# A chain of token mixers and feed-forward layers: the delta rule on raw keys and queries, a plain first chunk, wide projections

## The chip, the cores and the metric

The kernel runs on one core of one Trainium2 chip. The metric is the time of one execution on the device, in microseconds. Before the change it is 2003.51 us, the median of three runs (1998.67 to 2003.72).

## What is computed

The input is x, 256 tokens of 1024 channels in float32. Two layers of a first block are followed by two of a second block; each step is added to x after an RMS norm:

```python
for l in range(2):                       # first block
    x += 0.5 * swiglu(norm(x), ffa_w_in[l], ffa_w_out[l])          # d_ff = 2816
    x += mix(norm(x) @ w_in[l])          # MLA, gated delta rule (GDN), MoBA; gated sum @ w_out
    x += 0.5 * swiglu(norm(x), ffb_w_in[l], ffb_w_out[l])
for l in range(2):                       # second block
    x += even_mixer(norm(x)) if l == 0 else odd_mixer(norm(x))
    x += conv_glu(norm(x))               # silu(conv3(h @ w_gate)) * (h @ w_up) @ w_down
```

The delta rule has 4 heads of 128 and chunks of 64 tokens. q and k are normalised to length 1 (q is also scaled by 128 ** -0.5):

```python
a   = strict_lower((k * beta) @ k.T * decay)        # 64 x 64 in each chunk and head
u,w = solve(I + a, [v * beta, k * beta * exp(gcum)])
qk  = q @ k.T * decay
for each chunk: v_new = u - w @ state
                o     = (q * exp(gcum)) @ state + qk @ v_new
                state = state * exp(g_last) + (k * exp(g_last - gcum)).T @ v_new
o = rms_norm(o, out_norm) * silu(z)
```

The odd mixer has a linear recurrent unit (LRU) with a gelu gate, and dilated attention over 3 dilations and 4 heads of 64.

## The kernel before, in words

**Weights and products.** Weights come from HBM in chunks of up to 1 MB, one DMA each on SP's queue, into three staging buffers (`chunk`, L252). ScalarE rounds each piece of 1024 columns to a high part (L279) and VectorE subtracts for the low part (L280), into three buffers each. Every product with a weight is a sum of three: high*high, high*low, low*high. There are two forms:

- plain (`mm3`, L285; called by `gather_T` and `gather_nat`): three matmuls of 256 columns to one PSUM bank. `gather_T` makes channels by tokens, `gather_nat` tokens by channels, with x as the stationary operand and the weight's columns (256, or 212) as the moving one.
- paired (`gather_pair`, L405): x's high and low part stand side by side, so one matmul of 512 columns (L414) and one of 256 (L416) replace the three. The result lies in two halves of two banks; `whole` (L524) adds them with two ScalarE copies (L527) and two VectorE additions (L529).

PSUM has eight banks in two pools of four: `pa` for products with weights, `ps` for all else.

**Norms.** The update of x by a layer also makes the next layer's split x (`xx`, L361) and its squares. `stats` (L378) turns the sum of squares into 1/rms by a chain of small VectorE instructions (`rsqrt`, L311, three Newton steps) and spreads it over partitions with TensorE (`rows`, L343), as R. Results of products are multiplied by R afterwards, so the first products of a layer do not wait for it.

**Feed-forward** (`ffn`, L515). Eleven chunks of 256 channels: gate product, R, silu, up product, then the split into `gx`. The four swiglu layers use the paired form for gate and up, the two conv layers the plain one for gate and the paired one for up. `stats` comes after the first up product.

**The first block's mixer** (`mixer`, L658). The order in the program comes from generators: each `yield` is a step, and `_mix(main, fill, ratio)` (L185) puts `ratio` steps of filler behind each step of the main work. The order of each engine's queue follows from the program's order and a simulated timeline; only in the part from L727 is TensorE's order as written. The stages:

1. `mla_c` (L782): two products of 212 columns.
2. MLA's projections and heads, with `fill` (convolutions and projections of the GDN, gates) and `moba_proj` (L908: six products of 256 columns) as filler.
3. MoBA's four pairs of heads (`heads`, L613: logits `pL`, softmax, transposes `pPT`, output `pOT`), with what is left of `fill`, then `merge` of branch 0, then `gdn_keys` woven with the gates of branch 2 as filler, at 2.05 steps of filler for one (L697 to L709).
4. `gdn_invert` (L1124, the inverse of I + a in six levels), with `gdn_rest` woven with gates and merges as filler; `gdn_solve`; `gdn_scan` (L1202).

`gdn_keys` (L1026) turns the raw keys to tokens by channels (`pgk`), squares and sums them, makes 1/norm, multiplies (`kn`, L1046), transposes the normalised keys back (`pgkT`), copies them out (`knT`, L1051), and multiplies them with themselves (`pA`, L1073) and with the decay `Dn`, which holds beta. `gdn_rest` (L1076) does the same with the queries (`pgq`, `rsqrt`, `qn` L1099, `pgqT`, `gqT` L1111, `pQK`), and makes the right-hand sides `vb`, `kbe`, the state's keys `kde`, and the decayed queries (GpSimd L1112, `pgqd`).

**The odd mixer** (`odd`, L1436). Queries, keys and values take nine products of 256 columns (`qkv`, L1483). They are mixed with the LRU and with the transposes of q and k (`turn`). `dil_attn` (L1556: logits `pdL`, softmax, 18 transposes `pdPT` for each of two pairs, output `pdo`) then has the LRU's gate (`plg`) and the first two chunks of the output product (`pr`) as filler, at 0.3.

Of the kernel before, what the change touches and what calls it, by code (L numbers as in the profile page):

```python
# [40 lines left out]
def _rows(chunks, *kts):  # L41
# [9 lines left out]
    "w_in": _rows([[(0, 212)], [(212, 416), (1952, 1960)]]  # L51
                  + _runs((2472, 4008), (416, 1952), (1960, 2472), (4008, 7080)), 8),
# [8 lines left out]
    "od_w_in_2": _rows(_runs((0, 3328)), 8),  # L61
# [157 lines left out]
class _Net:  # L219
# [222 lines left out]

    def Rb(self, n=2, R=None):
        return (self.R if R is None else R).unsqueeze(1).to_broadcast([128, n, S])
# [70 lines left out]
    def ffn(self, gate, up, down, layer, scale, gain, conv=None):  # L515
        nc = self.nc
        v2 = lambda a: a.rearrange("p (b s) -> p b s", b=2)
        with ExitStack() as ctx:
# [13 lines left out]
            for c in range(11):  # L532
                if conv is None:
                    pg = self.proj_pair(*gate(c), self.pa, "pg")
                else:
                    pg = _all(self.proj_T(*gate(c), "pg"))
                if c == 0:
                    pu = self.proj_pair(*up(c), self.ps, "pu")
                    self.stats()
                if conv is None:  # L540
# [20 lines left out]
                g = whole(pu, "g")  # L561
                nc.vector.scalar_tensor_tensor(g, th, 0.5, g, op0=OP.mult, op1=OP.mult)
# [95 lines left out]
    def mixer(self, l, gain):  # L658
        pool = lambda ctx, name, bufs, **kw: ctx.enter_context(
            self.tc.tile_pool(name=name, bufs=bufs, reuse_waits="tile", **kw))  # L660
        with ExitStack() as ctx:
# [5 lines left out]
            with ExitStack() as c2:  # L667
# [29 lines left out]
                def keys():  # L697
                    yield from f
                    yield from self.merge(l, big, mg, 0, got["gate0"], brs[0])
                    yield from _weave(prep(), self.gates(l, big, got["gate2"], 2, 0))  # L700

                def prep():
                    got["D"] = self.gdn_decay(gk, got["scal"])
                    got["keys"] = yield from self.gdn_keys(gk, at, got[1], got["D"][0])
# [5 lines left out]
            with ExitStack() as c2:  # L710
                gp = pool(c2, "mxg", 1)
                scal = got["scal"]
                kn, knT, A = got["keys"]
# [3 lines left out]
                us = tiles("us")  # L717

# [8 lines left out]
                with self.tc.manual_schedule(engines={mybir.EngineType.PE}):  # L727
                    with ExitStack() as c3:
                        wk = pool(c3, "mxh", 1)
                        side = self.gdn_rest(out, wk, got, scal, got["D"][1], kn, knT)  # L730
# [4 lines left out]
                    with ExitStack() as c3:  # L735
                        brs[1] = _mix(self.gdn_scan(big, pool(c3, "mxj", 2), scal, out, us, got["sz"]), rest, 1.5)
# [45 lines left out]
    def mla_c(self, l, big):  # L782
        nc = self.nc
        csb = big.tile([128, 2, 424], F32, name="csb")
        ps = [_all(self.proj_nat("w_in", 28 * l + c, 212, "pc")) for c in range(2)]
        self.stats()
        for c in range(2):
            for t in range(2):
                nc.scalar.activation(csb[:, t, c * 212:(c + 1) * 212], ps[c][:, t * 212:(t + 1) * 212], AF.Copy,
                                     scale=self.rc[:, t:t + 1])  # L790
# [117 lines left out]
    def moba_proj(self, l, z):  # L908
        for i in range(3):
            for c in range(2):  # L910
                p = yield from self.proj_nat("w_in", 28 * l + W_MOBA + 2 * i + c, 256, "pmq")
                self.nat_heads(z[i][:, :, c * 256:(c + 1) * 256], p, 256)
# [70 lines left out]
    def gdn_decay(self, gp, scal):  # L983
# [16 lines left out]
        nc.vector.tensor_tensor(Dn, Dn, bc(beta), op=OP.mult)  # L1000
# [25 lines left out]
    def gdn_keys(self, gk, at, raw, Dn):  # L1026
# [3 lines left out]
        bch = lambda a: a.unsqueeze(2).to_broadcast([128, 4, 128])  # L1030
        ss = self.tiny.tile([128, 8], F32, tag="ss8", name="ss8")
        ps, kn, knT, A = [], [], [], []
        for t in range(2):
            ps.append(self.transposes("pgk", lambda h: raw[:, h, t * 128:(t + 1) * 128]))
# [4 lines left out]
        nc.vector.tensor_scalar(ss, ss, 0.25, EPS, op0=OP.mult, op1=OP.add)  # L1039
        r = self.rsqrt(ss, 8, "rl2")  # L1040
        nc.vector.tensor_scalar(r, r, 0.5, None, op0=OP.mult)
        for _ in range(4):
            yield
        for t in range(2):
            kn.append(gk.tile([128, 512], F32, name=f"kn{t}"))
            nc.vector.tensor_tensor(h4(kn[t]), h4(ps[t]), bch(r[:, 4 * t:4 * t + 4]), op=OP.mult)  # L1046
            yield
        for t in range(2):
            p = self.transposes("pgkT", lambda h: kn[t][:, h * 128:(h + 1) * 128])
            knT.append(gk.tile([128, 512], F32, name=f"knT{t}"))  # L1050
            nc.scalar.activation(knT[t], p, AF.Copy)  # L1051
            yield
        for t in range(2):
            p = self.ps("pA")
            self.inner(p, knT[t], knT[t])
# [4 lines left out]
        return kn, knT, A  # L1060
# [7 lines left out]
    def inner(self, p, a, b):  # L1068

        for h in range(4):  # L1070
            for c in range(2):
                s = slice(h * 128 + c * 64, h * 128 + c * 64 + 64)
                self.nc.tensor.matmul(p[64 * c:64 * c + 64, h * 64:h * 64 + 64], a[:, s], b[:, s],  # L1073
                                      start=True, stop=True)

    def gdn_rest(self, out, wk, raw, scal, Dt, kn, knT):  # L1076
# [3 lines left out]
        wq, kbe, kde, vb, qkT = out  # L1080
        h4 = lambda a: a.rearrange("p (h s) -> p h s", h=4)
        bch = lambda a: a.unsqueeze(2).to_broadcast([128, 4, 128])
        W = lambda nm: wk.tile([128, 512], F32, tag="gw", bufs=2, name=nm)
        f = self.tiny.tile([128, 2, 2, 4], F32, tag="gf", name="gf")
        ss = self.tiny.tile([128, 8], F32, tag="ss8", name="ssq")
        ps = []
        for t in range(2):
            ps.append(self.transposes("pgq", lambda h: raw[0][:, h, t * 128:(t + 1) * 128]))
            junk = W("gj")
            nc.scalar.activation(junk, ps[t], AF.Square)  # L1090
            nc.vector.reduce_sum(ss[:, 4 * t:4 * t + 4], h4(junk), axis=AX)
            yield
        nc.vector.tensor_scalar(ss, ss, 0.25, EPS, op0=OP.mult, op1=OP.add)
        r = self.rsqrt(ss, 8, "rq")
        nc.vector.tensor_scalar(r, r, 0.5 * 128 ** -0.5, None, op0=OP.mult)
        qn = []
# [631 lines left out]
```

## Time and profile before

| | |
|---|---|
| median of three runs | 2003.51 us |
| the profiled execution | 1998.36 us |
| its span, first to last instruction | 1996.6 us |
| TensorE busy | 1958.7 us (98%) |
| VectorE, ScalarE, GpSimd busy | 1537.9, 1102.9, 128.8 us |
| read from HBM | 323.87 MB |

A matmul's row has the length from its issue to its modelled end, with the pipeline in it; the distance between the starts of two matmuls that follow one another is what one costs in a full stream. An idle time is named behind the instruction that ended it, with what released it.

### The profile page before, as it was taken

What the parts mean: (1) busy time and instruction counts of PE and PEld (TensorE: products, weight loads), DVE (VectorE), ACT (ScalarE), POOL (GpSimd) and SP (SyncE); (2) the same over time, 40 slices, a digit from 0 to 9 for tenths busy, and PEclk for the clock granted to TensorE, in tenths of its full rate; (3) what the DMA queues carried; (4) which work ended last, traced back from release to release, by engine and by line L of the source; (5) the groups of instructions that cost most, each with busy time, mean ns of one, the idle gap of its engine ahead of it and who ended that gap; (6) DMA issues with size and microseconds to landing.
All of it is one profiled execution on the core that took longest, in us unless ns stands there. A gap on an engine that the chain in (4) does not pass through costs nothing.

```text
span 1996.6 us, 35914 instructions
## 1 busy us (share of the span) xinstructions
PE 1958.7 (98%) x14452; PEld 1799.1 (90%) x14452; DVE 1537.9 (77%) x2841; ACT 1102.9 (55%) x1812; POOL 128.8 (6%) x158
## 2 busy tenths in 40 slices
PE   7999999999999999999998999999999999999999
PEld 6889999799888988899997998889999999989998
DVE  6776899747877677768996587766978876978875
ACT  5555666435555555546663355555645655666653
POOL 0000030220000000001203100000000000020000
PEclk9999999999999999999999999999999999999999
DMA  6555544224555555555331255555244555426554
GB/s 239 190 185 186 175 148 148 105 66 158 180 190 179 194 176 190 181 186 180 130 146 69 102 172 187 184 180 185 106 148 169 190 177 201 168 63 220 183 179 137
DMA packets 50695, 327.24 MB, mean 164 GB/s; under 512 B 6624, under 2 KB 8672, under 8 KB 18528
## 3 DMA queue, kind: packets, MB, share of 16 engines
q1 hardware_dynamic: 49296, 324.09, 46.4%
q8 instruction: 113, 1.85, 0.4%
q10 hardware_dynamic: 1232, 0.85, 0.1%
q14 instruction: 54, 0.44, 0.1%
HBM read 323.87 MB, written 1.05 MB: 163 GB/s over the span
## 4 chain that ended last, share of the span: by engine, by line
PE 94%; DVE 3%; ACT 2%; issue 1%; DMA 0%; SPq 0%; DVEq 0%; ACTq 0%
PE pu L414 12%; PE pr L414 9%; PE pg L414 8%; PE pu L416 6%; PE pr L416 5%; PE pg L416 4%; PE pr L289 3%; PE pr L290 3%; PE pr L288 3%; PE pga L288 2%; PE pg L290 2%; PE pg L288 2%; PE pg L289 2%; PE pga L290 2%; PE pga L289 2%; PE pb L288 1%
## 5 line engine op out<-in xcount | busy, mean ns | idle before, releaser
L279 ACT ACTIVATE whi<-st 128x1024 fp32r<-128x1024 f32 (+2 forms) x628 | 651.0, 1037 | 695.4 <-PE pr L414 121.2
L280 DVE TENSOR_TENSOR wlo<-st,whi 128x1024 fp32r<-128x1024 f32 (+2 forms) x628 | 756.6, 1205 | 316.6 <-ACT whi L279 310.6
L414 PE MATMUL pu<-xx,whi 128*128 128x512 f32 x1056 | 372.5, 397 | 0.0
L416 PE MATMUL pu<-xx,wlo 128*128 128x256 f32 x1056 | 290.4, 280 | 0.0
L414 PE MATMUL pr<-gx,whi 128*128 128x512 f32 x792 | 272.7, 395 | 0.0
L414 PE MATMUL pg<-xx,whi 128*128 128x512 f32 x704 | 250.1, 399 | 11.3 <-ACT whi L279 11.3
L414 PEld LDWEIGHTS pu<-xx,whi 128*128 128x128 f32 x1056 | 196.3, 188 | 43.0
L416 PE MATMUL pr<-gx,wlo 128*128 128x256 f32 x792 | 211.2, 279 | 0.0
L416 PEld LDWEIGHTS pu<-xx,wlo 128*128 128x128 f32 x1056 | 199.4, 189 | 2.8
L416 PE MATMUL pg<-xx,wlo 128*128 128x256 f32 x704 | 194.4, 281 | 1.1 <-DVE wlo L280 1.1
L414 PEld LDWEIGHTS pr<-gx,whi 128*128 128x128 f32 x792 | 144.4, 188 | 29.7
L414 PEld LDWEIGHTS pg<-xx,whi 128*128 128x128 f32 x704 | 131.6, 189 | 41.2 <-ACT whi L279 12.0
L416 PEld LDWEIGHTS pr<-gx,wlo 128*128 128x128 f32 x792 | 149.3, 189 | 5.4
L416 PEld LDWEIGHTS pg<-xx,wlo 128*128 128x128 f32 x704 | 133.6, 190 | 4.7 <-DVE wlo L280 2.7
L288 PE MATMUL pga<-xx,whi 128*128 128x256 f32 x384 | 112.7, 293 | 0.0
L288 PE MATMUL pg<-xx,whi 128*128 128x256 f32 x384 | 109.3, 285 | 1.0 <-ACT whi L279 1.0
L290 PE MATMUL pg<-xx,wlo 128*128 128x256 f32 x384 | 109.3, 285 | 0.8 <-DVE wlo L280 0.8
L289 PE MATMUL pg<-xx,whi 128*128 128x256 f32 x384 | 109.1, 284 | 0.0
L289 PE MATMUL pga<-xx,whi 128*128 128x256 f32 x384 | 108.8, 283 | 0.0
L290 PE MATMUL pga<-xx,wlo 128*128 128x256 f32 x384 | 108.6, 283 | 0.0
L288 PEld LDWEIGHTS pg<-xx,whi 128*128 128x128 f32 x384 | 73.7, 192 | 2.2 <-ACT whi L279 1.2
L288 PEld LDWEIGHTS pga<-xx,whi 128*128 128x128 f32 x384 | 73.3, 191 | 2.4 <-issue 1.0
(563 smaller groups left out, 4547.2 us busy)
## 6 DMA issues: line engine op xcount, KB each, us to landing
st<-in_w_in_dram SPq DMA_DIRECT2D x52, 1024.0 KB, 4.8
st<-in_ffb_w_in_dram SPq DMA_DIRECT2D x44, 1024.0 KB, 4.8
st<-in_ffa_w_in_dram SPq DMA_DIRECT2D x43, 1024.0 KB, 4.9
st<-in_ffn_w_gate_dram SPq DMA_DIRECT2D x22, 1024.0 KB, 4.8
st<-in_ffn_w_up_dram SPq DMA_DIRECT2D x22, 1024.0 KB, 4.8
st<-in_ffa_w_out_dram SPq DMA_DIRECT2D x16, 896.0 KB, 4.5
st<-in_ffb_w_out_dram SPq DMA_DIRECT2D x16, 896.0 KB, 4.5
st<-in_ffn_w_down_dram SPq DMA_DIRECT2D x16, 896.0 KB, 4.6
```

Of the source, the lines that this page charges most:

```text
L279: self.hi = nc.scalar.activation(hi[:, :m], s, AF.Copy).ins
L280: nc.vector.tensor_tensor(lo[:, :m], s, hi[:, :m].bitcast(F32), op=OP.subtract)
L288: mm(out, a[0], b[0], start=start, stop=False, **kw)
L289: mm(out, a[0], b[1], start=False, stop=False, **kw)
L290: mm(out, a[1], b[0], start=False, stop=stop, **kw)
L414: mm(p, hi[:, k, c], x.rearrange("p e s -> p (e s)"), start=first == k0 + k, stop=False, skip_group_check=True)
L416: mm(p[:, S:], lo[:, k, c], x[:, 0, :], start=False, stop=last == k0 + k, skip_group_check=True)
```

## The change

- **Delta rule.** Keys and queries are no longer normalised. `a` and `qk` are products of the raw, transposed convolution results; 1/|k|^2 * beta multiplies the rows of `Dn`, 1/|k| * beta goes into `vb`, 1/|k|^2 * beta * exp(gcum) into `kbe`. The queries' length goes into the epsilon of the output's norm (`vq`, two small matmuls and a copy). The transposes `pgkT` and `pgqT` with their copies, the products L1046 and L1099, the queries' `rsqrt` and GpSimd's L1112 go; a copy of the raw keys (`kr`), a reciprocal, and a product out of PSUM for the decayed queries (`qd`) come. `inner` runs before the query transposes.
- **Order in stage 3.** `gdn_keys` is woven with merge 0 and then the gates, and not with the gates alone.
- **Plain first chunk.** Chunk 0 of each `ffn` uses the plain form for gate and up (six up products and four gate products), into one `pa` bank each.
- **Wide projections.** `wide_nat` makes 424 or 512 columns at a time, one bank for each half of the tokens: for `mla_c`, `moba_proj` and two of three products of each `qkv`. Weights are laid out in chunks of 4 rows of blocks by 512 columns.
- **Odd mixer.** The LRU's gate is mixed with the transposes of k; the values' products move into the filler of `dil_attn`, at 1.0, and must be done before its first output product.

The diff, cut to its core:

```diff
+    def wide_nat(self, name, i, cols, nm="pn"):
+        ps = [self.pa(nm) for _ in range(2)]
+        for j in range(2):
+            for k0, kk, hi, lo in self.chunk(name, i + j):
+                for t in range(2):
+                    for k in range(kk):
+                        m = 4 * j + k0 + k
+                        x = [a[:, t * 128:(t + 1) * 128] for a in self.xs(m)]
+                        self.mm3(ps[t][:, :cols], x, (hi[:, k, :], lo[:, k, :]), m == 0, m == KD - 1)
+                    yield
+        return ps
...
             for c in range(11):
-                if conv is None:
+                pair = conv is None and c > 0
+                if pair:
                     pg = self.proj_pair(*gate(c), self.pa, "pg")
                 else:
                     pg = _all(self.proj_T(*gate(c), "pg"))
                 if c == 0:
-                    pu = self.proj_pair(*up(c), self.ps, "pu")
+                    pu = _all(self.proj_T(*up(c), "pu"))
                     self.stats()
...
                     yield from f
-                    yield from self.merge(l, big, mg, 0, got["gate0"], brs[0])
-                    yield from _weave(prep(), self.gates(l, big, got["gate2"], 2, 0))
+                    yield from _weave(prep(), _chain(self.merge(l, big, mg, 0, got["gate0"], brs[0]),
+                                                     self.gates(l, big, got["gate2"], 2, 0)))
...
-        ps = [_all(self.proj_nat("w_in", 28 * l + c, 212, "pc")) for c in range(2)]
+        ps = _all(self.wide_nat("w_in", 28 * l, 424, "pc"))
...
-            for c in range(2):
-                p = yield from self.proj_nat("w_in", 28 * l + W_MOBA + 2 * i + c, 256, "pmq")
-                self.nat_heads(z[i][:, :, c * 256:(c + 1) * 256], p, 256)
+            ps = yield from self.wide_nat("w_in", 28 * l + W_MOBA + 2 * i, 512, "pmq")
...
     def gdn_keys(self, gk, at, raw, Dn, beta):
...
-            nc.scalar.activation(junk, ps[t], AF.Square)
+            nc.scalar.activation(junk, p, AF.Square)
+            nc.scalar.activation(kr[t], p, AF.Copy)
             nc.vector.reduce_sum(ss[:, 4 * t:4 * t + 4], h4(junk), axis=AX)
             yield
-        r = self.rsqrt(ss, 8, "rl2")
...
-            nc.vector.tensor_tensor(h4(kn[t]), h4(ps[t]), bch(r[:, 4 * t:4 * t + 4]), op=OP.mult)
-            yield
-        for t in range(2):
-            p = self.transposes("pgkT", lambda h: kn[t][:, h * 128:(h + 1) * 128])
...
+        nc.vector.tensor_scalar(ss, ss, 4 * EPS, None, op0=OP.add)
+        nc.vector.reciprocal(r2, ss)
+        nc.vector.tensor_tensor(r2, r2, fl(beta), op=OP.mult)
+        nc.vector.tensor_tensor(Dn, Dn, r2.unsqueeze(2).to_broadcast([128, 8, 64]), op=OP.mult)
+        yield
         for t in range(2):
             p = self.ps("pA")
-            self.inner(p, knT[t], knT[t])
+            self.inner(p, raw, raw, t)
...
+        r = self.rsqrt(ss, 8, "rl2")
+        nc.vector.tensor_tensor(rb, r, fl(beta), op=OP.mult)
...
     def gdn_rest(...):
+        for t in range(2):
+            p = self.ps("pQK")
+            self.inner(p, raw[1], raw[0], t)
...
+            p = self.transposes("pgq", lambda h: raw[0][:, h, t * 128:(t + 1) * 128])
+            nc.scalar.activation(junk, p, AF.Square)
+            nc.vector.tensor_tensor(h4(qd[t]), h4(p), bch(egc[:, t, :]), op=OP.mult)
...
+        p = self.ps("pvq")
+        for c in range(2):
+            nc.tensor.matmul(p[half(c), 0:8], self.ident[:, half(1 - c)], ss, start=True, stop=True)
+        nc.vector.tensor_copy(vq, p[:, 0:8])
...
     def odd(self, gain):
             _mix(qkv(0, q), core, 0.5)
-            for i, z in ((1, k), (2, v)):
-                turned = turn(i - 1, (q, k)[i - 1], (qT, kT)[i - 1])
-                _mix(qkv(i, z), _chain(turned, core), (0, 0.5, 0.2)[i])
-                _all(turned)
+            turned = turn(0, q, qT)
+            _mix(qkv(1, k), _chain(turned, core), 0.5)
+            _all(turned)
             _all(core)
-            fill = _chain(lru_gate(), lru_out())
-            _mix(self.dil_attn(wk, dil, qT, kT, v, yh, yl, (q, k)), fill, 0.3)
+            turned = turn(1, k, kT)
+            _mix(lru_gate(), turned, 0.5)
+            _all(turned)
+            values = qkv(2, v)
+            fill = _chain(values, lru_out())
+            _mix(self.dil_attn(wk, dil, qT, kT, v, yh, yl, (q, k), values), fill, 1.0)
```

## Rows read from the trace of the kernel before

**Rows 1.** The page: engines' busy time, and the chain that ended last.

```profile
PE 1958.7 (98%) x14452; PEld 1799.1 (90%) x14452; DVE 1537.9 (77%) x2841; ACT 1102.9 (55%) x1812; POOL 128.8 (6%) x158
...
PE 94%; DVE 3%; ACT 2%; issue 1%; DMA 0%; SPq 0%; DVEq 0%; ACTq 0%
```

**Rows 2.** Waits of TensorE: who waited for whom, total us, times, longest.

```profile
PE pA L1073 <- ACT knT L1051: 6.3, 3, 3.0
...
PE pT L1136 <- DVE qn L1099: 1.2, 1, 1.2
PE prow L348 <- DVE rc L389: 1.1, 2, 0.5
```

**Rows 3.** Timeline of TensorE, plain form and mla_c: 256 columns, then 212.

```profile
198.81 0.28 PE L288 MATMUL pr<-gx,whi 128*128 128x256 f32 x1
198.93 0.28 PE L289 MATMUL pr<-gx,whi 128*128 128x256 f32 x1
...
199.17 0.26 PE L288 MATMUL pc<-whi,xx 128*128 128x212 f32 x1
...
209.88 0.52 PE L383 MATMUL pst<-ones,sqacc 128*128 128x1 f32 x4
210.25 0.36 PE L288 MATMUL pga<-xx,whi 128*128 128x256 f32 x1
```

**Rows 4.** Timeline of TensorE: 512 columns, and a step of the paired form.

```profile
247.58 0.40 PE L289 MATMUL pkv<-wlo,ch 128*128 128x512 f32 x1
247.81 0.40 PE L290 MATMUL pkv<-whi,cl 128*128 128x512 f32 x1
...
711.50 0.40 PE L414 MATMUL pg<-xx,whi 128*128 128x512 f32 x1
...
711.85 0.40 PE L414 MATMUL pg<-xx,whi 128*128 128x512 f32 x1
```

**Rows 5.** Timeline of TensorE, end of stage 3, layer 0.

```profile
370.84 0.92 PE L300 MATMUL pL<-qkT 64*128 64x128 f32 x6
...
374.71 1.04 PE L1065 MATMUL pgkT<-C,kn 128*128 128x128 f32 x8
378.75 0.69 PE L1073 MATMUL pA<-knT 128*64 128x64 f32 x16 [3.00 <-ACT knT L1051]
...
382.08 1.27 PE L602 MATMUL pPT<-C,pr 128*128 128x128 f32 x6
384.01 0.43 PE L297 MATMUL pOT<-PT,mv 128*64 128x256 f32 x1 [0.65 <-ACT PT L604]
...
384.81 0.39 PE L1136 MATMUL pF<-C,gF 64*64 64x64 f32 x6
```

**Rows 6.** Timeline of ScalarE in the same stretch.

```profile
376.80 0.47 ACT L604 ACTIVATE PT<-pPT 128x384 f32<-128x384 f32 x1
```

**Rows 7.** Windows: granted clock (PEclk) after the waits; columns us, engines, PEclk, DMA.

```profile
379.53:382.94 3.41, 3.19 (x28) 2.48 (x29) 1.12 (x3) 0.55 (x2) 2.25 (x4) 0.50 0.00 0
...
1062.20:1065.60 3.40, 3.31 (x40) 2.56 (x40) 1.67 (x3) 1.04 (x3) 1.35 (x2) 0.50 0.02 5
...
1512.80:1516.10 3.30, 3.30 (x18) 3.30 (x17) 0.00 (x0) 0.00 (x0) 0.00 (x0) 0.50 0.07 30
...
1773.90:1788.40 14.50, 11.34 (x98) 8.34 (x96) 10.54 (x23) 10.22 (x25) 2.78 (x2) 1.00 0.19 55
```

**Rows 8.** Chain that ended last: one group of four transposes in gdn_rest.

```profile
402.57 0.59 PE pgqT L1065 x4
```

**Rows 9.** Timeline, second chunk of a swiglu and of conv_glu: waits of TensorE.

```profile
30.32 0.73 PE L414 MATMUL pg<-xx,whi 128*128 128x512 f32 x2 [1.03 <-ACT whi L279]
...
31.58 0.38 PE L416 MATMUL pg<-xx,wlo 128*128 128x256 f32 x1 [0.52 <-DVE wlo L280]
...
1510.58 0.39 PE L288 MATMUL pg<-xx,whi 128*128 128x256 f32 x1 [1.03 <-ACT whi L279]
...
1511.84 0.39 PE L290 MATMUL pg<-xx,wlo 128*128 128x256 f32 x1 [0.76 <-DVE wlo L280]
```

More of the change, by code (lines that the diff above doesn't have):

```diff
@@ L60 @@
     "ev_w_out_2": [(c, (k, 4)) for k in (0, 4) for c in _OUT],
-    "od_w_in_2": _rows(_runs((0, 3328)), 8),
+    "od_w_in_2": _rows(_runs((0, 1024)), 8)
+                 + [x for c in range(1024, 3328, 768)
+                    for x in _rows([[(c, c + 512)]], 4, 4) + _rows(_runs((c + 512, c + 768)), 8)],
     "od_w_out_2": [(c, (k, n)) for k, n in ((0, 4), (4, 2)) for c in _OUT],
@@ L537, in ffn @@
                 if c == 0:
-                    pu = self.proj_pair(*up(c), self.ps, "pu")
+                    pu = _all(self.proj_T(*up(c), "pu"))
                     self.stats()
-                if conv is None:
+                if conv is None and not pair:
+                    zz = wk.tile([128, 2, S], F32, tag="z", name="z")
+                    nc.vector.tensor_tensor(zz, v2(pg), self.Rb(), op=OP.mult)
+                elif pair:
                     zz = whole(pg, "z")
@@ L712, in mixer @@
                 scal = got["scal"]
-                kn, knT, A = got["keys"]
+                kr, rs, A = got["keys"]
                 tiles = lambda nm, n=512: [gp.tile([128, n], F32, name=f"{nm}{t}") for t in range(2)]
@@ L729, in mixer @@
                         wk = pool(c3, "mxh", 1)
-                        side = self.gdn_rest(out, wk, got, scal, got["D"][1], kn, knT)
+                        side = self.gdn_rest(out, wk, got, scal, got["D"][1], kr, rs, vq)
                         M = _mix(self.gdn_invert(pool(c3, "mxi", 2), A), _weave(side, rest), 0.65)
@@ L1059, in gdn_keys @@
             yield
-        return kn, knT, A
+        r = self.rsqrt(ss, 8, "rl2")
+        nc.vector.tensor_tensor(rb, r, fl(beta), op=OP.mult)
+        yield
+        return kr, (r2, rb), A
     def transposes(self, nm, src):
@@ L1066, in transposes, with inner, gdn_rest @@
         return p
-    def inner(self, p, a, b):
+    def inner(self, p, a, b, t):
         for h in range(4):
             for c in range(2):
-                s = slice(h * 128 + c * 64, h * 128 + c * 64 + 64)
-                self.nc.tensor.matmul(p[64 * c:64 * c + 64, h * 64:h * 64 + 64], a[:, s], b[:, s],
+                s = slice(t * 128 + c * 64, t * 128 + c * 64 + 64)
+                self.nc.tensor.matmul(p[64 * c:64 * c + 64, h * 64:h * 64 + 64], a[:, h, s], b[:, h, s],
                                       start=True, stop=True)
-    def gdn_rest(self, out, wk, raw, scal, Dt, kn, knT):
+    def gdn_rest(self, out, wk, raw, scal, Dt, kr, rs, vq):
         nc = self.nc
@@ L1486, in qkv @@
                 for g in range(3):
-                    p = yield from self.proj_nat("od_w_in_2", 4 + 3 * i + g, 256, "pd")
-                    self.nat_heads(z[:, g], p, 256)
+                    if g == 0:
+                        ps = yield from self.wide_nat("od_w_in_2", 4 + 3 * i, 512, "pd")
+                        for t in range(2):
+                            nc.scalar.activation(z[:, 0:2, t, :], v2(ps[t]), AF.Copy, scale=self.rc[:, t:t + 1])
+                    elif g == 2:
+                        p = yield from self.proj_nat("od_w_in_2", 6 + 3 * i, 256, "pd")
+                        self.nat_heads(z[:, g], p, 256)
                     if i == 2:
@@ L1602, in dil_attn @@
                     yield
+            _all(values)
             po = self.ps("pdo")
```

102 lines of the change are left out of this document (43 added, 59 removed).

## The prediction, made before the changed kernel ran

> **What bounds the kernel now.** The page first: TensorE is busy for 98% of the span, and the chain that ended last runs through it for 94% [rows 1]. So the time is TensorE's work, plus the places where it waits. VectorE (77%) and ScalarE (55%) count only where TensorE waits for them, and DMA has no share in the chain: the bytes stay the same, so transfers are costed at nothing, covered by products that outlast them. Next, the waits of TensorE: few and short, but the longest of the ones inside the kernel belong to the part that changes, 6.3 us for `knT`, then 1.2 for `qn` and 1.1 for `rc` [rows 2]. Last, the timeline, for what one matmul costs (distance between starts): 0.12 us for 256 columns, and (209.88 - 199.17) / 96 = 0.112 for 212 [rows 3]; 0.23 for 512, and 0.35 for a paired step, which does the work of three plain matmuls [rows 4]. The price goes with columns, so fewer, wider matmuls save little each.
>
> The sum below is made against the profiled execution, 1998.4 us. The median of the three runs shown is 5.1 us above it; I keep that distance. What a measurement of this kernel can tell from no change is 0.3%, 6 us.
>
> **The change, part by part.**
>
> *Wide projections.* `mla_c`: 96 matmuls of 0.112 become 48 of 424 columns. Between 256 columns at 0.12 and 512 at 0.23 a straight line gives 0.194 (bounds: 0.193 at the price per column of 512, 0.199 at that of 256) [rows 3, 4]. So 10.7 - 9.3 = 1.4 us a layer (1.2 to 1.5). `moba_proj`: 288 matmuls of 0.12 become 144 of 0.233, 1.0 us a layer; the odd mixer's three pairs of narrow products lose as much, 1.0. Sum 2 x 2.4 + 1.0 = -5.8. The number of DMAs, pieces and splits stays; evacuations get fewer, and lie under products. Two banks are now held at once, of four in `pa`; nothing else uses `pa` then.
>
> The Trainium skill ("TensorE: Matmul & The Clock Gate", section "Back-to-back issue gap" and the one on LDWEIGHTS) gives columns / 2.4 ns plus 2.5 for a full stream, and 107 ns to load 128 columns of weights. The rows of 212 columns (112 ns) agree with the load as their bound; those of 256 and 512 (120, 233) lie above 109 and 216, so the measured ones are used. By the page this part would be an estimated 2 x (1.7 + 0.4) + 0.4 = 4.6 us.
>
> *Transposes.* In stage 4 two groups of `pgqT` go in each layer, 0.59 us each in the chain [rows 8], and eight `pgkT` in stage 3, 0.88 for the eight (1.04 less the pipeline's 0.16, which is a plain row's 0.28 over its cost of 0.12) [rows 3, 5]. What comes is one small group (`pvq`); the nearest is `pst`, 0.37 from its start to the next matmul [rows 3]. -1.18 - 0.88 + 0.37, for two layers -3.4 (bounds -3.0 to -4.1). The reciprocal, the copy `kr`, the product `qd` and the `rsqrt` that stays lie on VectorE and ScalarE beside products; what is late by them is A, now needed only at `gdn_invert`, several microseconds on.
>
> *The wait for the keys.* `pgkT` starts at 374.71 and `pA` at 378.75: 4.04 us with 0.88 of work. Behind it `pA` waits again (0.31 named) [rows 5]. The cause is a queue: `knT`'s copy stands on ScalarE behind the last pair's exponentials. With raw keys `pA` depends on convolutions that were done long before, so 3.5 us a layer go (6.3 of both are named as idle in [rows 2], the rest is pipeline). What is late next: output and transposes of the last two pairs of heads, whose copy `PT` stands in the same queue until 377.3 [rows 6]. There is also less filler: by my count of yields 39 steps stand behind 27 steps of heads in place of 45, so at 2.05 the filler ends at step 20 and not 22, two steps behind the last pair's logits. That is some 3 steps of 1.4 us (12 matmuls of 0.12), against 6.4 us from the last logits' start (370.84) to the end of that copy. I put a new wait at 0.8 us (0 to 3). After the old wait TensorE was granted 1.2 GHz for 3.4 us, in both layers (0.50 in two windows of [rows 7]), so half of 3.4 us was lost. Taken as gone in one layer of two: -0.9 a layer (0 to -1.7). Together -3.6 a layer, -7.2 (bounds -1 to -10.4).
>
> *The wait for the queries.* `gdn_invert` waits for VectorE, which is in the queries' `rsqrt` and `qn`: 1.2 us named [rows 2], and its transposes hold up what is behind them for about as long again. No such chain is left at the start of `gdn_rest`: -2 (0 to -3). GpSimd's L1112 goes too, off the path.
>
> *Plain first chunk.* TensorE pays: 16 x (3 x 0.12 - 0.35) = 0.16 us for each of ten products, +1.6. In return two ScalarE copies and two VectorE additions go for each from queues that hold up the second chunk's split. That wait: 1.03 + 0.52 in a swiglu, twice alike, and 1.03 + 0.76 in conv_glu [rows 9], with 1.1 for `rc` in the two others [rows 2]; 6.0 us in all, and 1.7 for the half clock that follows in conv_glu [rows 7]. The second chunk is still paired, and its own copies stand in these queues, so I take half, -3.8. The banks are now held until R is there; chunk 1 takes the other two of `pa`, chunk 2 needs those of chunk 1, which don't wait for R. Net -2.2 (bounds +1.6 to -6.1).
>
> *Odd mixer.* In 1773.9 to 1788.4 TensorE is busy 11.3 of 14.5 us [rows 7]: transposes and outputs of dilated attention, whose filler is used up. Values' products fill that now, except for the end of the second pair; the new point is `pdo`, which waits for the last values' copy, and k's transposes, which have 2.9 us of gate products ahead where they had more. Of 3.2 us I take -2 (+2 to -3.2).
>
> *New waits.* Every stage is ordered anew. A wait of the size of the one in conv_glu, 1.8 us [rows 9], is added once: +1.8 (0 to +8, four of them with a half clock in one).
>
> Sum: -5.8 - 3.4 - 7.2 - 2 - 2.2 - 2 + 1.8 = -20.8; said as -20. 1998.4 - 20 = 1978.4 for a profiled execution, 1983.5 for the median.
>
> **The rivals.**
>
> *A, all waits go.* Each term at its better bound: -5.8 - 4.1 - 10.4 - 3 - 6.1 - 3.2 = -32.6, 1971. For: all these waits have a named cause that the diff removes. Against: ScalarE's and VectorE's queues stay full. 0.13.
>
> *B, waits only move.* TensorE's work alone counts: -5.8 - 3.4 + 1.6 = -7.6, 1996. For: the heads' last softmax ends hardly earlier than before, and the last pairs stand in the same ScalarE queue [rows 6]. Against: `pA` has no input left that is late. 0.17.
>
> *C, the filler runs out under the last pair* (slower). Place: the end of stage 3. From `pL` at 370.84 to `pF` at 384.81 are 14 us, with some 4 us of the heads' own work [rows 5]. With no products behind that `pL`, softmax, copies and output would lie bare: about 10 us a layer. It decides if the filler ends before step 18, some four steps earlier than counted, which the reordering by simulated times can do. Then +20 in place of the -7.2 of the keys: -20.8 + 7.2 + 20 = +6.4, 2010. 0.07.
>
> *D, nothing is left.* B with new waits of 7 us, as the reorder of four stages could make: 2003. 0.03.
>
> **How the numbers follow.** The forecast has 0.60, with 1975 to 1993 as its own range. Faster by over 0.3% (under 1997.5): nearly all of it, A, and half of B: 0.59 + 0.13 + 0.08 = 0.80. Within 0.3%: the other half of B, D, and 0.01: 0.13. Slower: C, 0.07. The range goes from a little below A, 1969, to 1999, past B; C and D, an end of B and an end of A are left out.
>
> **What would show it.** Right: no row of TensorE waiting for `knT` or `qn`; `pc` at about 0.19 us from start to start, `pmq` at 0.23; no window at 0.50 behind stage 3; first chunks of `ffn` with three matmuls of 256 columns and a shorter wait at the second chunk; `pdPT` between products `pd`. TensorE's busy share at 98% or above, with a shorter span. Wrong: waits of `pOT` or `pPT` for `PT` or `pr` at the end of stage 3 over 3 us a layer (C), a wait of `pdT` for k or of `pdo` for v, a wait at the second chunk as long as before (B), or 424 columns at over 0.2 us.

## The result, and the profile after

| | before | after |
|---|---|---|
| median | 2001.37 us | 1977.71 us (1975.25 to 1978.92) |
| profiled execution, its span | 1998.36, 1996.6 us | 1975.25, 1973.4 us |

The ratio is 0.9881, with 0.9861 to 0.99 as its interval: faster by 1.2%. The fourth run of the kernel before brings its median from 2003.51 to 2001.37. A run of 6534.83 us is left out of the median of experiment 8. The predicted median was 1983.5. Of the 5.8 us between, 3.1 lie in the profiled execution (1978.4 forecast, 1975.25 measured); the rest is the distance from there to the median, which the prediction kept at 5.1 us and which is 2.5 here.

The page of the changed kernel, its engines and the chain that ended last (beside [rows 1]):

```profile
PE 1937.5 (98%) x14060; PEld 1772.7 (90%) x14060; DVE 1530.1 (78%) x2797; ACT 1091.0 (55%) x1766; POOL 122.8 (6%) x154
...
PE 94%; DVE 4%; issue 1%; ACT 1%; DMA 0%; SPq 0%; DVEq 0%; ACTq 0%
```

TensorE still bounds it. Its busy time fell by 21.2 us and the span by 23.2, so little of the gain is idle time. But matmuls at half clock count as busy, and so do matmuls that follow one another a little more slowly; the stages have to be asked. The table gives, for each, the time from the start of its first matmul to that of the next stage's first, in the timelines of the two profiled executions (together some -23.5; the first stage starts 0.4 later); "predicted" is the sum of the prediction's terms that fall there.

| stage | before | after | change | predicted |
|---|---|---|---|---|
| feed-forward layers (six) | | | -11.9 | -2.2 |
| of these, the swiglu behind mixer 0, its gate and up part | 125.9 | 123.5 | -2.4 | |
| `mla_c` to the first gate, two layers | 22.17 | 19.32 | -2.85 | -2.8 |
| first gate to last head (stages 2 and 3), two layers | 348.8 | 335.6 | -13.1 | -11.0 |
| inversion, solve and scan, to the end of the mixer, two layers | 245.8 | 248.9 | +3.0 | -3.6 |
| even mixer, whose code is unchanged | 112.3 | 109.5 | -2.8 | 0 |
| odd mixer | 119.2 | 123.2 | +4.0 | -3.0 |
| new waits, in no named place | | | | +1.8 |

The total was nearly met by parts that missed in both directions. The waits of TensorE, in the view used for [rows 2], from the second on:

```profile
PE pdPT L1627 <- DVE dpr L1614: 3.9, 1, 3.9
PE pOT L299 <- ACT PT L625: 3.9, 4, 1.4
PE pb L290 <- ACT brh L307: 3.2, 2, 1.6
...
PE pb L291 <- DVE brl L308: 1.2, 2, 0.6
...
PE prow L350 <- DVE rc L391: 0.3, 1, 0.3
```

No row has `knT` or `qn`, and `rc` fell from 1.1 to 0.3. Three kinds of wait are new or longer: for the softmax of dilated attention (`dpr`), for the transposed probabilities at the heads' end (`PT`, 1.3 us in two waits before), and for the delta rule's own output (`brh`, `brl`). Their places are, in layer 0 of the timeline of TensorE, the heads' end, where [rows 5] stood, then the scan's end, and in the odd mixer the first transposed probability:

```profile
371.18 0.49 PE L623 MATMUL pPT<-C,pr 128*128 128x128 f32 x3
372.80 0.43 PE L299 MATMUL pOT<-PT,mv 128*64 128x256 f32 x1 [1.13 <-ACT PT L625]
...
375.17 0.43 PE L299 MATMUL pOT<-PT,mv 128*64 128x256 f32 x1 [0.69 <-ACT PT L625]
...
375.97 1.15 PE L1155 MATMUL pF<-C,gF 64*64 64x64 f32 x32
...
464.56 0.74 PE L290 MATMUL pb<-brh,whi 128*128 128x256 f32 x4 [1.60 <-ACT brh L307]
...
1743.58 0.70 PE L299 MATMUL pdL<-kT,qT 64*128 64x256 f32 x2 [0.15 <-DVE dmx L1602]
1748.69 0.45 PE L1627 MATMUL pdPT<-C,dpr 128*128 128x128 f32 x1 [3.94 <-DVE dpr L1614]
```

The windows of the changed kernel show the granted clock behind two of these waits (0.50, which is 1.2 GHz), none behind the heads, and what the engines did before the wait for `dpr`:

```profile
465.70:469.10 3.40, 3.20 (x15) 3.20 (x16) 0.14 (x1) 0.00 (x0) 0.00 (x0) 0.50 0.10 39
...
1745.70:1755.90 10.20, 5.51 (x24) 5.14 (x25) 8.47 (x28) 5.85 (x15) 0.00 (x0) 0.50 0.07 26
371.20:376.00 4.80, 2.98 (x29) 1.87 (x27) 3.71 (x6) 3.21 (x6) 0.00 (x0) 1.00 0.63 218
...
1733.00:1745.00 12.00, 11.60 (x85) 8.74 (x85) 12.00 (x27) 8.64 (x14) 5.34 (x3) 1.00 0.27 89
```

In the last row the third pair after the length is VectorE: busy for 12.00 of 12.00 us. But it does not work on the softmax alone. Three rows of its timeline, from the last 5 us before the wait ends:

```profile
1743.92 2.43 DVE L1688 TENSOR_TENSOR_SCAN lh<-la,lb 128x256 f32<-128x256 f32 x4
1746.27 0.14 DVE L1612 RECIPROCAL dsm<-dsm 128x2 f32<-128x2 f32 x1
...
1748.13 0.94 DVE L1614 TENSOR_SCALAR dpr<-dpr,dsm 128x384 f32<-128x384 f32 x2
```

The scan belongs to the LRU, and so do two products (L1552) that stand, with one more row of logits, between the reciprocal and the division that TensorE waits for. In VectorE's order as it is, `dpr` came as early as it could; with another one, up to 1.7 us between the reciprocal's end (1746.41) and the division might have gone. No run tried that. The heads' tail at 371.2 is thin too (2.98 of 4.8 us), yet the clock stayed.

The wide form, `mla_c` of layer 0:

```profile
198.61 0.36 PE L290 MATMUL pc<-whi,xx 128*128 128x424 f32 x1
...
205.89 0.50 PE L385 MATMUL pst<-ones,sqacc 128*128 128x1 f32 x4
206.25 0.44 PE L291 MATMUL pc<-wlo,xx 128*128 128x424 f32 x1
...
208.27 0.28 PE L290 MATMUL pga<-xx,whi 128*128 128x256 f32 x1
```

Up to `pst`, which now stands among them, 38 matmuls take 7.28 us: 0.192 each, next to the 0.194 of the prediction's line and just under its bounds (0.193 to 0.199). All 48 with `pst` take 9.66 us, where 96 with `pst` behind them took 11.08 (199.17 to 210.25 in [rows 3]): 1.42 us less. The Trainium skill ("TensorE: Matmul & The Clock Gate", section "Back-to-back issue gap") would give an estimated 0.179; this trace does not agree, and the line through measured widths came nearer.

### The profile page after: what moved, and what is told of

Same layout as the page of the kernel before. It is cut to its first block, busy times and chain, and to the rows that moved or that the text cites. A ratio compares the mean times of both kernels' runs of the same rounds, so it can differ in the third digit from the quotient of the medians.

```text
span 1973.4 us, 35062 instructions
## 1 busy us (share of the span) xinstructions
PE 1937.5 (98%) x14060; PEld 1772.7 (90%) x14060; DVE 1530.1 (78%) x2797; ACT 1091.0 (55%) x1766; POOL 122.8 (6%) x154
## 4 chain that ended last, share of the span: by engine, by line
PE 94%; DVE 4%; issue 1%; ACT 1%; DMA 0%; SPq 0%; DVEq 0%; ACTq 0%
PE pu L416 11%; PE pr L416 9%; PE pg L416 7%; PE pu L418 6%; PE pr L418 5%; PE pg L418 4%; PE pg L292 3%; PE pg L291 3%; PE pg L290 3%; PE pr L291 3%; PE pr L290 3%; PE pr L292 3%; PE pga L290 3%; PE pga L291 2%; PE pga L292 2%; PE pb L291 1%
## 5 line engine op out<-in xcount | busy, mean ns | idle before, releaser
L416 PE MATMUL pu<-xx,whi 128*128 128x512 f32 x960 | 336.8, 395 | 0.0
L418 PE MATMUL pu<-xx,wlo 128*128 128x256 f32 x960 | 264.1, 279 | 0.0
L416 PE MATMUL pg<-xx,whi 128*128 128x512 f32 x640 | 223.6, 394 | 0.0
L416 PEld LDWEIGHTS pu<-xx,whi 128*128 128x128 f32 x960 | 178.8, 188 | 39.3
L418 PEld LDWEIGHTS pu<-xx,wlo 128*128 128x128 f32 x960 | 180.8, 188 | 1.6
L416 PEld LDWEIGHTS pg<-xx,whi 128*128 128x128 f32 x640 | 119.2, 188 | 26.7
L290 PE MATMUL pg<-xx,whi 128*128 128x256 f32 x448 | 128.0, 286 | 9.6 <-ACT whi L281 9.6
L291 PE MATMUL pg<-xx,whi 128*128 128x256 f32 x448 | 127.6, 285 | 0.0
L418 PEld LDWEIGHTS pg<-xx,wlo 128*128 128x128 f32 x640 | 120.2, 188 | 1.1
L292 PEld LDWEIGHTS pg<-xx,wlo 128*128 128x128 f32 x448 | 86.5, 193 | 1.0 <-DVE wlo L282 0.8
```

The lines of the kernel that those rows point to most:

```text
L290: mm(out, a[0], b[0], start=start, stop=False, **kw)
L291: mm(out, a[0], b[1], start=False, stop=False, **kw)
L292: mm(out, a[1], b[0], start=False, stop=stop, **kw)
L416: mm(p, hi[:, k, c], x.rearrange("p e s -> p (e s)"), start=first == k0 + k, stop=False, skip_group_check=True)
L418: mm(p[:, S:], lo[:, k, c], x[:, 0, :], start=False, stop=last == k0 + k, skip_group_check=True)
```

## The experiments

Parts are undone in 1 to 5 and 8, single numbers changed in 6, 7, 9 and 11; 10 joins two, and 12 makes one part alone. Ratios are to the kernel before on the same chip; the changed kernel's 0.9881 is the mark. "Own stages" means the change in the stages that the edit touches, against the profile of the changed kernel. One profile stands behind each kernel, and the last section shows that a stage can differ by 2.8 us between two profiles of the same code.

**1. The odd mixer's order as before** (wide products kept).

```diff
-            turned = turn(1, k, kT)
-            _mix(lru_gate(), turned, 0.5)
...
-            fill = _chain(values, lru_out())
+            fill = _chain(lru_gate(), lru_out())
```

> The changed kernel, with the odd mixer's order as before (its wide products stay). Theory: the new order costs time, because filler is spent ahead of dilated attention's softmax, TensorE then waits 4 us for VectorE and runs at half clock for 10 us (5 us lost), so going back gains 3 to 7 us over the changed kernel: about 1973 us, ratio to before 0.984 to 0.987, and no window at 0.50 behind the logits. Rival (the step of the prediction): the new order saves about 2 us, so going back gives about 1980, ratio 0.989 to 0.991.

Measured: 1976.36 us, ratio 0.9877 (0.9862 to 0.9892), between the two. Its own stage fell by 3.7 us (123.2 to 119.5), but more was given back in stages that the edit doesn't touch: the even mixer took 112.3 us instead of 109.5, with two windows at 0.50, and the first feed-forward layer 2.3 more; the inversion to the mixers' ends took 1.0 less. The last feed-forward layer took 1.1 more. So the new order costs time in its own place, and the median alone does not show it.

**2. The first chunk paired again**, gate and up, in all layers (`ffn` as before).

```diff
-                pair = conv is None and c > 0
+                pair = conv is None
...
-                    pu = _all(self.proj_T(*up(c), "pu"))
+                    pu = self.proj_pair(*up(c), self.ps, "pu")
```

> The changed kernel, with the first chunk of every feed-forward layer paired again. Theory: the plain form took the waits at the second chunk away, so they come back (about 2 us in two layers, under 1 us in two, near 2 us and a half clock in conv_glu), less 1.6 us of TensorE work: 1982 to 1985 us, ratio 0.990 to 0.992, and rows of pg waiting for whi near 30 and 690 us. Rival: the waits left for another reason (order, stages ahead), the form only costs its 1.6 us: about 1976, ratio 0.987 to 0.988.

Measured: 1991.19 us, ratio 0.9948 (0.9935 to 0.996): the part is worth far more than either theory said. Two of its waits of TensorE, in the view of waits:

```profile
PE pg L416 <- ACT whi L281: 11.1, 3, 9.0
...
PE prow L350 <- DVE rc L391: 1.4, 3, 0.5
```

9.0 of the first row is the kernel's start, which the changed kernel has as well (9.6); 2.1 and 1.4 us of waits don't make 13 us. The feed-forward stages grew by 13.0 us, mostly without a wait in any row. Experiment 12 takes this up.

**3. The old delta rule, the new weave kept**, and **4. narrow projections** (212 and 256 columns, weights laid out as before).

> The changed kernel, with the delta rule on normalised keys and queries as before; the keys stay woven with merge 0 and the gates. Theory: the keys' wait is a matter of the chain norm, transpose, copy, product. It comes back at least in part, and so do 1.7 us of transposes a layer and the wait for the queries: 1983 to 1989 us, ratio 0.990 to 0.994. Rival: the earlier place alone (merge 0 behind it) hides that chain, so only the transposes and the queries' wait return, less the wait at merge 1 that the change brought: 1978 to 1982, ratio 0.987 to 0.990.

> The changed kernel, with 212 and 256 columns in place of the wide projections. Theory: cost by columns, 5.8 us in all: about 1983.5 us, ratio 0.990 to 0.9925; 0.112 us from start to start in mla_c. Rival (the page on the clock gate): about 4.6 us less per its formula, 1982; a second rival, that narrow products are hidden by waits next to them: 1978, ratio 0.988.

Measured: 1986.43 us, ratio 0.9922 (0.9909 to 0.9936), and 1987.94 us, ratio 0.9941 (0.9928 to 0.9954). In the fourth, the theory's 5.8 us was passed: own stages grew by 10.0 us: 2.8 in `mla_c`, 2.9 in stages 2 and 3 (1.5 a layer, where `moba_proj` is), 4.3 in the odd mixer; the last is more than its narrow matmuls cost, since in the new order k comes later there (a wait of `pdT` for k, 2.3 us, which the changed kernel lacks).

The third is the surprise. The number is the theory's, its chain is not: with normalised keys but the merge woven between the keys' steps, no wait for `knT` is left. The windows at the end of stage 3 of its two layers show what is:

```profile
378.10:384.90 6.80, 6.22 (x58) 4.61 (x58) 4.51 (x7) 1.94 (x5) 3.43 (x4) 0.50 0.00 1
1053.90:1060.70 6.80, 6.22 (x61) 4.32 (x61) 4.22 (x7) 2.10 (x5) 3.14 (x4) 0.50 0.01 2
```

**5. The merge in front of the keys again**, raw keys kept.

```diff
-                    yield from _weave(prep(), _chain(self.merge(l, big, mg, 0, got["gate0"], brs[0]),
-                                                     self.gates(l, big, got["gate2"], 2, 0)))
+                    yield from self.merge(l, big, mg, 0, got["gate0"], brs[0])
+                    yield from _weave(prep(), self.gates(l, big, got["gate2"], 2, 0))
```

> Only the place of the steps goes back: the gate merge of branch 0 (32 matmul triples) stands again in front of the keys' steps, not woven between them; the new delta rule on raw keys stays. Theory (raw keys take the whole wait away, because the product for A now needs only the conv output, so the place does not matter): no wait at the A product, 1975 to 1980, ratio 0.987 to 0.990, equal to the changed kernel within 0.1%. Rival (half of the keys' gain was the place: the chain squares, reciprocal, scaling of Dn is still late for A's eviction and the steps without fill at the end of the heads are more now): 1981 to 1985, ratio 0.990 to 0.992.

Measured: 1985.92 us, ratio 0.9938 (0.9922 to 0.9954). The theory fell: the place matters. The rival named the right sign and the wrong chain. The timeline of TensorE at the heads' end, and the windows there:

```profile
374.99 0.53 PE L299 MATMUL pOT<-PT,mv 128*64 128x256 f32 x1 [2.05 <-ACT PT L625]
...
378.44 0.69 PE L299 MATMUL pOT<-PT,mv 128*64 128x256 f32 x1 [0.58 <-ACT PT L625]
```

```profile
375.20:382.00 6.80, 6.22 (x58) 4.37 (x56) 4.35 (x9) 2.27 (x5) 0.73 (x1) 0.50 0.45 155
1054.40:1061.20 6.80, 6.22 (x62) 4.48 (x60) 4.50 (x9) 2.27 (x5) 1.45 (x2) 0.50 0.46 157
```

The product for A waits nowhere, so either edit alone, raw keys or the weave, removes the named wait. But in both half-way kernels the first wait for `PT` is longer (2.05 here and 1.85 in experiment 3, against 1.13 in the changed kernel), and 6.8 us behind it run at half clock in each layer. Stages 2 and 3 took 170.9 us in layer 0 with the weave alone, 170.6 with raw keys alone, 167.7 with both. With neither it was 174.6, but in that kernel `moba_proj` was narrow too; less the 1.5 us of experiment 4 that is an estimated 173.1. So either edit alone saves some 2 us, and the second one some 3 more, which is about the half of 6.8 that the clock takes. The inversion to the mixers' ends took 3.8 us more than in the changed kernel, with a half-clock stretch at the scan's end of both layers (the changed kernel has one in layer 0), though nothing was edited there.

**6. One merge step held back** for the scan's end.

```diff
-                        M = _mix(self.gdn_invert(pool(c3, "mxi", 2), A), _weave(side, rest), 0.65)
+                        M = _mix(self.gdn_invert(pool(c3, "mxi", 2), A), _weave(side, rest), 0.62)
```

> One number: the fill steps per step of the inversion go from 0.65 to 0.62, so 18 instead of 19 are used there and one merge step is left for the end of the scan, as in the kernel before. Theory (the side chain has one step less since the change, so one merge step too many is spent under the inversion and the merge of the last branch meets its late output: 4.4 us of waits in two layers, one of them with 3.4 us at the half clock, i.e. 1.7 lost): those waits go, 1972 to 1975, ratio 0.985 to 0.987. Rival (the wait comes from the longer chain of the output norm itself, or the inversion pays what the scan wins): 1976.5 to 1979, ratio 0.987 to 0.990.

Measured: 1971.96 us, ratio 0.9867 (0.9854 to 0.988), at the lower edge of the theory. Its interval overlaps the changed kernel's (0.9861 to 0.99), so the waits and the stages have to show it. The waits of TensorE, from the second on; `pb` is not among them, and what the rival feared (`pNM`) grew by 1.1 us:

```profile
PE pdPT L1627 <- DVE dpr L1614: 3.9, 1, 3.9
PE pOT L299 <- ACT PT L625: 3.6, 4, 1.1
PE pNM L1155 <- DVE gM L1188: 2.1, 4, 0.5
```

Inversion, solve and scan, to the end of the mixer, fell by 5.8 us in two layers (by 4.8 against experiment 1, which has the changed kernel's code there). The first layer and the even mixer, both unedited, took 3.4 us more. `gdn_rest` yields once less than it did, so 0.65 spent one step of `rest` too early, and the merge ran into its own late input.

**7. 1.7 instead of 2.05 fill steps per step of the MoBA heads.**

```diff
-                brs[2] = _mix(self.heads(big, at, *self.moba_heads(at, *z), sc, nsc), f2, 2.05)
+                brs[2] = _mix(self.heads(big, at, *self.moba_heads(at, *z), sc, nsc), f2, 1.7)
```

> One number: the fill steps per step of the MoBA heads go from 2.05 to 1.7, so the keys, merge and gate steps last until nearly the end of the heads instead of ending seven steps earlier. Theory (what is late at the heads' end since the change is the transposed probabilities, 3.9 us in four waits, because the fill, 8 steps a layer shorter, has run out): these waits shrink to under 1.5 us and nothing replaces them, 1974 to 1976, ratio 0.986 to 0.988. Rival (the fill is only moved: the steps taken from the earlier heads leave the same waits there, or the A product comes so late that the inversion waits for it): 1977 to 1981, ratio 0.988 to 0.990.

Measured: 1986.86 us, ratio 0.9939 (0.9927 to 0.9952), worse than the rival. The waits for `PT` shrank as expected, from 3.9 to 1.7 us in all, but VectorE has A's last steps late, and the inversion waits (timeline of TensorE):

```profile
381.70 1.15 PE L1155 MATMUL pT<-gM,gF 64*64 64x64 f32 x32 [2.53 <-DVE gM L1174]
```

Own stages grew by 2.1 us. The rest of the distance lies in stages that the edit doesn't touch: 4.7 in the even mixer, 2.2 in the first layer.

**8. Only the gate of the first chunk paired** (one line of experiment 2).

> The first chunk of the three plain feed-forward layers has its gate half paired again; its up half stays plain. With both halves paired the kernel took 13.5 us more than the changed one, of which the visible waits explain under 7. Theory A (the gain is the up half: the wait for the eviction of the first paired up product, behind the statistics, is what goes, and the paired stream then settles in its fast rhythm of 5.55 us per 32 matmuls): 1976 to 1980, ratio 0.987 to 0.990, fast rhythm in at least two of the three later layers. Theory B (any paired work before the statistics spoils the rhythm, 5.65 us per 32, about 2 us a layer in three layers, and brings the wait for the gate's eviction back): 1984 to 1991, ratio 0.992 to 0.995, slow rhythm in most layers.

Measured: 1982.8 us, ratio 0.992 (0.9907 to 0.9934). The median lies between the two ranges, but two of the three later layers kept the fast rhythm, as A has it, and 2.9 us of the distance are in the even mixer. The feed-forward layers (the edit touches the first one too) took 3.5 us more than in the changed kernel, where experiment 2 has 13.0: by these stages most of the part is the up half.

**9. As 6, and 1.5 instead of 1.0 fill steps in dilated attention**; **10. as 6, and the odd order of before**; **11. as 9, and 1.9 instead of 2.05** for the MoBA heads.

> The held-back merge step of the run before (0.62 under the inversion) and one more number: 1.5 instead of 1.0 fill steps per step of the dilated attention, so nine instead of six steps of values and output projection stand in front of the first transposed probability. Theory (in the changed kernel TensorE stands 4.2 us there, because VectorE is busy for all of the 12 us before with the softmax, and then 10.2 us run at the half clock; with more TensorE work in front the wait is covered and the clock stays): that wait falls under 1.5 us, no half-clock stretch there, 4 to 7 us less than the held-back kernel's 1972, 1965 to 1968, ratio 0.983 to 0.985. Rival (the later steps, with less fill, wait for the probabilities instead, or VectorE's evictions of the fill delay the softmax): 1970 to 1974, ratio 0.985 to 0.988.

> The held-back merge step (0.62) and the odd mixer's order as before the change. Theory (the new odd order costs 3.6 us in its own stretch, 123.2 against 119.6 us; the equal medians of that kernel and the changed one came from half-clock stretches in the even mixer, whose code is the same in both): 1967 to 1970, ratio 0.983 to 0.986. Rival (the odd order is neutral in all, the half clock only turns up elsewhere): 1971 to 1974, ratio 0.986 to 0.988.

> As the first kernel of this call (0.62 and 1.5), and 1.9 instead of 2.05 fill steps per step of the MoBA heads. With 1.7 the waits of the heads' end halved, from 3.9 to 1.7 us, but the inversion's first steps waited 4.2 us for VectorE. Theory (half of the shift takes part of the first and little of the second, since the A product ends some two steps before the heads do): 1 to 2 us less than the first kernel of this call. Rival (the inversion's wait begins with any shift, since VectorE's work on A is only moved later): 1 to 4 us more than it.

Measured: 1972.89, 1970.89 and 1977.54 us; ratios 0.9869 (0.9853 to 0.9884), 0.9848 (0.9835 to 0.9861), 0.9887 (0.9873 to 0.9901). The ninth left the wait for `dpr` at 3.9 us and the half clock behind it, since the order of TensorE's instructions up to that wait came out the same: it follows from a simulated timeline there, and the number alone did not move it. It does not test the theory. In the tenth that wait is gone, as its waits of TensorE show from the second on, with 1.4 us each for `pdo` and `pdL` in its place:

```profile
PE pOT L299 <- ACT PT L625: 3.6, 4, 1.1
PE pNM L1155 <- DVE gM L1188: 2.1, 4, 0.5
PE pr L290 <- ACT yh L310: 1.6, 1, 1.6
PE pdo L299 <- ACT k L1626: 1.4, 2, 0.7
PE pdL L299 <- DVE dmx L1599: 1.4, 1, 1.4
```

Its odd mixer took 3.6 us less than in experiment 6, the layer behind 1.1 more, and the even mixer 1.3 more. It has the lowest median of all: 1.5% under the kernel before. Its interval ends where the changed kernel's begins and overlaps those of 6 and 9, so against these it is not clear of noise. In the eleventh the theory fell again: stages 2 and 3 grew by 1.8 and 3.3 us against the ninth, with 6.8 us at half clock in layer 1. Both smaller ratios, 1.7 and 1.9, were worse than the changed kernel's 2.05; larger ones were not tried.

**12. The plain first chunk alone**, put into the kernel before (the opposite of experiment 2, alone).

> The plain first chunk alone, put into the kernel before; everything else stays as it was there. Theory (the plain chunk takes the waits at the start of the feed-forward layers, and the paired stream behind it settles in the rhythm of 5.55 us per 32 matmuls instead of 5.65, wherever it stands): the two layers behind the mixers fall from 125.9 to 123.5 to 123.8 us each and stay in the fast rhythm, the convolution's layer behind the even mixer, which has no paired work, is not touched, 1992 to 1996, ratio 0.996 to 0.998. Rival (the 13.5 us that undoing this part cost were mostly half-clock stretches elsewhere and the rhythm comes by chance): 1997 to 2001, ratio 0.9985 to 1.0005, the two layers not both fast. Second rival (the part is worth the whole 13.5 us by itself): 1986 to 1989, ratio 0.993 to 0.9945.

Measured: 1987.75 us, ratio 0.9939 (0.9927 to 0.9952): the second rival, the whole worth by itself. The feed-forward layers took 11.3 us less than in the kernel before. The expectation had a fault: the convolution's layers do have paired up products, and the one behind the even mixer fell from 130.1 to 126.5 us. The two swiglus fell from 125.9 to 123.5 and 123.7, as the theory said. A stretch of paired steps in the timeline of TensorE, kernel before, then this one, eight steps apart:

```profile
549.85 0.40 PE L414 MATMUL pu<-xx,whi 128*128 128x512 f32 x1
...
552.66 0.40 PE L414 MATMUL pu<-xx,whi 128*128 128x512 f32 x1
```

```profile
549.66 0.39 PE L414 MATMUL pu<-xx,whi 128*128 128x512 f32 x1
...
552.44 0.39 PE L414 MATMUL pg<-xx,whi 128*128 128x512 f32 x1
```

Eight steps take 2.81 and 2.78 us. A product of 16 steps takes 5.65 us in the one rhythm and 5.55 in the other, and the twenty products behind the first chunk keep theirs to the end of the layer: 2 us a layer with no wait to be seen.

## Why the prediction was right, point by point

**Wide projections (-5.8)** held in sum, and in `mla_c` by the mechanism: 0.192 us a matmul for 0.194, 1.4 us a layer. `moba_proj` gave more, 1.5 us a layer for 1.0, if experiment 4 is taken for it. In the odd mixer the 1.0 depends on the order: with the order of before, wide products took 119.5 us (experiments 1 and 10) and narrow ones 119.2, so nothing was gained; in the new order narrow products cost 4.3, the wait for k included. Undoing all widths cost 10.0 in own stages, so the parts don't add up one by one.

**Transposes and the keys' wait (-0.9 and -3.6 a layer)** came out at about the right size for stages 2 and 3 (-13.1 against -11.0; `moba_proj` is about 1 of the 2.1). The cause, a queue, is shown by experiment 3, where the wait goes although `knT` stays: the weave brings the first copy to 371.81, ahead of the last pair's exponentials (from 374.22), where it stood behind them before (378.12). The half clock, taken as gone in one layer of two, went in both. The new wait at the tail was put at 0.8 us a layer; the row says 3.9 in all, 1.3 of which were there before: 1.3 new ones a layer. Rival C did not come, and rival B's mark, TensorE's work alone, was passed. Experiments 3 and 5 showed that the two edits save the clock only together.

**The queries' wait (-2)** went, but the step "No such chain is left at the start of `gdn_rest`: -2" looked at one end only. The side chain became a step shorter, the filler at fixed ratios moved earlier, and two layers paid 4.4 us in `pb`, with a half clock behind it in layer 0, at the scan's end. The sum had +1.8 for a wait of this sort, without a place. Experiment 6 shows the place.

**Plain first chunk (net -2.2)** is the term that was most off: -11.9. The step that was too small is "I take half, -3.8": nearly all the second chunk's waits went, the one of `conv_glu` with its half clock (3.6 us there), and no chunk behind waited instead. Most of the rest is the rhythm of the paired stream, priced at one value, 0.35 a step, from a layer that had the fast one [rows 4]; the two swiglus behind the mixers had the slow one, 2 us each.

**Odd mixer (-1 and -2)** had the wrong sign: +4.0. The step that failed is "Values' products fill that now": they ran out, TensorE stood 3.9 us for a softmax that stood in VectorE's queue between steps of the LRU, and 10.2 us at half clock followed. The price of the new point, `pdo`, was looked at; the one of `pdPT` was not.

**The even mixer (0)** gave 2.8 us by the clock in unchanged code. That is luck, not a gain of the change: experiment 1, with the changed kernel's code up to there, took 112.3 us again. With this the errors (-9.7 in the feed-forward layers, -2.1 in stages 2 and 3, +6.6 behind them, +7.0 in the odd mixer, -2.8 here, and -1.8 for the wait in no named place) come to about -3, and the forecast was good by cancelling as much as by its steps.

## What to carry to other kernels

When a chain gets a step shorter, every fixed ratio of fill that runs beside it must be counted again to its far end: a merge step spent too early cost more than the queries' wait had. A wait may cost its own length and the clock behind it; two edits that each shorten a thin stretch may save the clock only together, so that undoing them one by one is no sum. Read each edit in its own stages, since here unchanged stages differ by several microseconds from profile to profile.

## What the runs showed of the hardware

The paired stream has two rhythms. In the gate and up products of the three swiglu layers behind the first one, 32 matmuls took 5.55 us in 32 of the 33 layers whose first chunk was plain (the changed kernel, experiments 1, 3 to 7 and 9 to 12), in two of the three of experiment 8, and in one of the six with a paired first chunk (the kernel before and experiment 2); in the others they took 5.65. In the first layer, where the kernel starts, a plain first chunk gave the fast one in three kernels of eleven, one with a paired gate in one of three (the kernel before, experiments 2 and 8). There the code does not decide it: the changed kernel and experiment 1 have the same instructions in the same order on all four engines up to the odd mixer, and their first layers had the fast and the slow rhythm (189.0 and 191.3 us). The rhythm is settled in the first chunks and kept to the layer's end. What sets it was not tried further and stays open.

The same code met the clock differently from profile to profile. The changed kernel and experiment 1 differ only from the odd mixer on; the first has a half-clock stretch at the scan's end of layer 0 (125.1 us from the inversion to the mixer's end, against 124.0) and none in the even mixer (109.5 against 112.3). The ninth and the tenth, measured on one chip, have the same instructions up to the odd mixer too. A thin stretch of their even mixers, some 97 us in, ran at full clock in the ninth (first row) and at half in the tenth (second row):

```profile
1452.40:1459.20 6.80, 6.30 (x52) 6.30 (x53) 2.58 (x5) 1.87 (x4) 0.14 (x2) 1.00 0.60 248
```

```profile
1452.40:1459.20 6.80, 5.90 (x28) 5.89 (x28) 1.46 (x3) 0.00 (x0) 0.14 (x2) 0.50 0.66 275
```

That stage took from 109.5 us (after, and experiments 4, 9, 11) to 114.2 (experiment 7). So its clock is not set by the code of the kernel alone; what else sets it was not settled.
